# A hybrid attention block on one core: copies, ALiBi rows, a modulation sum, weight splits and the last output tile put elsewhere

## The chip, the cores and the metric

The kernel runs on one core of a Trainium2 chip. The metric is the device time of one execution in microseconds, taken as the median of several runs. Before the change it is 679.64 us, the median of three runs (677.84, 679.64, 680.59).

## The reference, cut to what matters

One transformer block on a sequence of 512 rows of width 1024, all in float32. A modulation vector is made from `c`; the mixer has six forget-gate attention heads ("fox"), four mLSTM heads and six block-sparse heads with ALiBi slopes ("moba"); then a gated feed-forward of width 2816.

```python
mod = silu(c) @ w_ada + b_ada
sh1, sc1, g1, sh2, sc2, g2 = split(mod, 6)
hn = rms(x, norm1_g) * (1 + sc1) + sh1
fq, fk, fv, ff, mq, mk, mv, mi, mf, mo, bq, bk, bv = split(hn @ w_in)
logf = log_sigmoid(f_pre); cum = cumsum(logf)      # fox and mLSTM gates
mq, mk = split(silu(causal_conv(concat(mq, mk))))
y = concat(fox(fq, fk, fv, cum), mlstm(mq, mk, mv, gates), moba(bq, bk, bv, slopes))
x = x + g1 * (y @ w_out)
hn = rms(x, norm2_g) * (1 + sc2) + sh2
gate, up = split(hn @ w_gate_up)
x = x + g2 * ((silu(gate) * up) @ w_down)
```

## The kernel before, in words

Every float32 product is made of three matmuls in a rounded type (fp32r): each operand is split into a high part (a copy into that type, usually on ACT) and a low part (the operand minus its high part, on DVE or on GpSimd, called POOL), and `mm3` (line 207) adds high x high, high x low and low x high. A name that ends in h or l is such a part. `wload` (line 235) loads a weight tile through SP's DMA queue, makes the high part on ACT and the low part on the engine that it is given. Stage buffers for weights rotate through four, split buffers through six.

**Stage 0** (lines 251 to 399) normalises `x`, makes the first modulation and the projection `gT[0..3]` of the mLSTM q|k channels. Its last lines copy the four PSUM banks to `qkz[0..3]`, in turn on ACT and DVE (lines 395 to 399).

**The mixer** (lines 401 to 986) is a list of groups of projection steps, written by `add_group` (line 410): A (mLSTM values and gates), F0, F1, F2 (fox), B0 to B2 (moba), E (output gate) and o0 (output projection). Each group has eight weight tiles `kt` and four row tiles `t`, one PSUM bank for each row tile; four banks with the tag "g" rotate, so that the first matmuls of F0 write the banks that group A used. A bank of A is empty when `after_a` (line 498) has read it: the gate sum into `gt` and, for two tiles `Vm0` and `Vm1`, a high part on ACT and a low part on DVE. The low part of a weight tile goes to POOL for `kt` in `WPG = (0, 2, 4, 6)`, except in group A (line 414).

Between these steps a queue of attention work runs: `plan_mlstm` and `plan_softmax`. What mLSTM needs first is the **gate chain**: `gates_1` (line 505, log-sigmoid as a row of small DVE steps on `gtmp` with an exponential on ACT, ending in `pre`), `gates_2` (cumulative sums `pF` on TensorE, then `Fc` and `ar` on DVE), `gates_3` (transpose `pR`, copy `rr`, running maximum `Mr`, and the table `RW` with high and low rows), and from `RW` the matmul `mb` that spreads a row over 128 partitions, from which the decay tiles `E` are made. `ms` and `mo` are the mLSTM score and value products.

`ada_all` (line 603) is a generator that makes later modulations beside this work: g1 (line 604, two halves named g10 and g11), sc2, sh2. Each half is eight loads of 128x512 and eight DVE steps that add a load times a column of `cs` to an accumulator (lines 566 to 581). `row_constants` (line 483) makes `sel` (a 0/1 table, built on POOL, cast on DVE) and the ALiBi rows `AL` (a DMA, a copy on ACT, a subtraction on DVE); it is called once, ahead of the step loop (line 929).

In this part the program order is not the order of issue: a scheduler places the instructions of every engine by their dependences, and each engine then runs its own list strictly in that order. `V, S, G, TE, SY` are thin wrappers (`_InOrder`, line 104) that can also chain instructions by hand.

**The second half** (from line 989) is the last output projection, the second norm and the feed-forward, and then the down projection `d`: two column halves of 512, four row tiles each, 22 weight tiles (line 1320 on). For the last four weight tiles the loop runs row tile by row tile, and after each row tile DVE multiplies the bank by `g1b` (here g2), adds `x1` and SP stores it. For the very last row tile these two DVE steps and the store are done in two halves of 256 columns, after all its matmuls.

Of the kernel before, what the change touches and what calls it, by code (L numbers as in the profile page):

```python
# [11 lines left out]
AF = mybir.ActivationFunctionType  # L12
# [46 lines left out]
DLAST = 4  # L59
# [44 lines left out]
class _InOrder:  # L104


    def __init__(self, tc, eng, on):
        self._tc, self._eng, self._on, self._last = tc, eng, on, None

    def __getattr__(self, name):  # L110
        f = getattr(self._eng, name)

        def call(*a, **k):
            r = f(*a, **k)  # L114
            ins = getattr(r, "ins", None)
            if ins is None or not self._on[0]:
                self._last = None
            else:
                if self._last is not None:
                    self._tc.add_manual_dep(  # L120
                        ins, self._last.name,
                        mybir.DependencyInfo(mybir.DependencyClass.NoSync, mybir.DependencyReason.DATA),
                        reason="issue order")
                self._last = ins
            return r

        return call
# [3 lines left out]
def hybrid_block_kernel(  # L131
# [75 lines left out]
    def mm3(o, ah, al, wh, wl, start, stop):  # L207
        TE.matmul(o, ah, wh, start=start, stop=False)
        TE.matmul(o, ah, wl, start=False, stop=False)
        TE.matmul(o, al, wh, start=False, stop=stop)  # L210
# [40 lines left out]
    with ExitStack() as s0:  # L251
# [143 lines left out]
        for m in range(4):  # L395
            if m % 2:
                V.tensor_copy(qkz[m], gT[m])
            else:
                S.activation(qkz[m], gT[m], AF.Copy)
# [10 lines left out]
    def add_group(name, kts, srcf, n, lhs, after, blk=BLK):  # L410
        box = {}

        def load(kt):
            box["w", kt] = wload(srcf(kt), n, f"{name}w{kt}", G if kt in WPG and name != "A" else V)
# [68 lines left out]
    def row_constants():  # L483
# [7 lines left out]
        V.tensor_copy(sel[0:64], sv)  # L491
# [74 lines left out]
    def ada_half(c0, name, bias):  # L566
        acc = adp.tile([P, 512], F32, tag="aacc", name=name, bufs=1)
        for k in range(8):
            s_ = adp.tile([P, 512], F32, tag="ast", name=f"{name}s{k}", bufs=AST)
            SY.dma_start(s_, w_ada_v[:, k, c0:c0 + 512])  # L570
            if k == 0:
                V.tensor_scalar(acc, s_, cs[:, 0:1], None, op0=ALU.mult)
            else:
# [357 lines left out]
    def g12():  # L931
        gs["lf"] = gates_1()

# [10 lines left out]
    for i in range(3):  # L944
# [3 lines left out]
             len(steps) - len(OKT) + 2: [load_x1]}  # L948
# [371 lines left out]
    for hf_ in range(2):  # L1320
        gg = [bank(tg, f"d{hf_}{t}") for t, tg in enumerate(("gggg", "sstt")[hf_])]

        def down(j, t, hf_=hf_, gg=gg):
# [9 lines left out]
            mm3(gg[t], ah[:, tsl], al[:, tsl], wh, wl, j == 0, j == NJ - 1)  # L1333
# [4 lines left out]
        for t in range(NT):  # L1338
            for j in range(NJ - DLAST, NJ):
                down(j, t)  # L1340
            parts = 2 if hf_ and t == NT - 1 else 1
            for c_ in range(parts):
                n = 512 // parts
                o = slice(c_ * n, c_ * n + n)
                ho = slice(512 * hf_ + c_ * n, 512 * hf_ + c_ * n + n)
# [43 lines left out]
```

## Time and profile before

| | before |
|---|---|
| median of three runs | 679.64 us |
| the profiled execution | 678.59 us |
| its span, first to last instruction | 676.8 us |
| TensorE matmul busy | 646.9 us, 96% |
| DVE busy | 518.1 us, 77% |
| ACT busy | 365.1 us, 54% |
| POOL busy | 97.2 us, 14% |
| mean granted TensorE clock | 0.995 |

The span counts from the first to the last instruction on the core; the execution's time has some 2 us more around it. Busy time of TensorE is modelled from pipelined matmuls. In the rows below, a name stands for all tiles of that name with their numbers left out (`F` for F0 to F2, `g` for g10 and g11, `E`, `ms`, `mo` for all heads); all program lines appear as L114, the wrapper's line. `PE` is TensorE, `PEld` its weight loads. A note in brackets at a row's end is the idle time ahead of it and what ended it.

### The profile page before, as it was taken

What the parts mean: (1) busy time and instruction counts of PE and PEld (TensorE: products, weight loads), DVE (VectorE), ACT (ScalarE), POOL (GpSimd) and SP (SyncE); (2) the same over time, 40 slices, a digit from 0 to 9 for tenths busy, and PEclk for the clock granted to TensorE, in tenths of its full rate; (3) what the DMA queues carried; (4) which work ended last, traced back from release to release, by engine and by line L of the source; (5) the groups of instructions that cost most, each with busy time, mean ns of one, the idle gap of its engine ahead of it and who ended that gap; (6) DMA issues with size and microseconds to landing.
All of it is one profiled execution on the core that took longest, in us unless ns stands there. A gap on an engine that the chain in (4) does not pass through costs nothing.

```text
span 676.8 us, 11779 instructions
## 1 busy us (share of the span) xinstructions
PE 646.9 (96%) x4238; PEld 588.9 (87%) x4238; DVE 518.1 (77%) x1034; ACT 365.1 (54%) x722; POOL 97.2 (14%) x135
## 2 busy tenths in 40 slices
PE   4999899999999999999999999999999999999997
PEld 3678888899999988778999999999999998788885
DVE  3549889969998899888778987888777999448313
ACT  4445478656876777645834554554544665316210
POOL 3012216344252355000000000000000000000000
PEclk9999988999999999999999999999999999999999
DMA  9986736667877667621346433322433237306101
GB/s 270 306 244 166 189 94 145 169 176 205 199 219 180 177 197 189 222 87 33 109 156 219 125 125 125 113 60 78 125 125 126 100 120 225 148 15 214 51 0 62
DMA packets 95549, 99.64 MB, mean 147 GB/s; under 512 B 8186, under 2 KB 70010, under 8 KB 95492
## 3 DMA queue, kind: packets, MB, share of 16 engines
q1 hardware_dynamic: 95492, 98.91, 50.3%
q8 instruction: 33, 0.54, 0.4%
q14 instruction: 24, 0.20, 0.1%
HBM read 84.15 MB, written 2.10 MB: 127 GB/s over the span
## 4 chain that ended last, share of the span: by engine, by line
PE 64%; DVE 19%; ACT 5%; DMA 5%; issue 4%; SPq 2%; POOL 0%; DVEq 0%; ACTq 0%; POOLq 0%
PE d L114 14%; PE B L114 5%; PE F L114 4%; PE ol L114 3%; PE gT L114 2%; DVE g L114 2%; SPq L114 2%; PE f9A L114 1%; PE f8A L114 1%; PE f7A L114 1%; PE f6A L114 1%; PE f5A L114 1%; PE f4A L114 1%; PE f3A L114 1%; PE pc L114 1%
## 5 line engine op out<-in xcount | busy, mean ns | idle before, releaser
L114 ACT ACTIVATE ah<-A 128x512 fp32r<-128x512 f32 x44 | 25.6, 620 | 33.4 <-PE d L114 33.1
L114 DVE TENSOR_TENSOR al<-A,ah 128x512 fp32r<-128x512 f32 x44 | 29.1, 685 | 18.1 <-ACT ah L114 18.1
L114 DVE TENSOR_TENSOR r<-r,r 128x1024 f32<-128x1024 f32 x20 | 24.4, 1220 | 1.5 <-DMA r<-in_w_gate_up_dram 1.2
L114 DVE TENSOR_TENSOR fo<-d,g1b 128x512 f32<-128x512 f32 (+1 forms) x9 | 5.6, 630 | 17.9 <-PE d L114 17.8
L114 ACT ACTIVATE Fp<-Fs,Fmn 128x128 f32<-128x128 f32 (+3 forms) x24 | 12.6, 526 | 9.8 <-DVE Fmn L114 5.6
L114 ACT ACTIVATE u<-u 128x512 f32<-128x512 f32 x20 | 12.5, 627 | 8.1 <-DVE u L114 8.0
L114 ACT ACTIVATE Bp<-Bs,Bmn 128x128 f32<-128x128 f32 (+3 forms) x24 | 12.6, 526 | 7.4 <-DVE Bmn L114 3.5
L114 DVE SCALAR_TENSOR_TENSOR m<-pc,b1sc,prmT 128x1 f32<-128x1 f32 x8 | 1.7, 218 | 19.1 <-PE pc L114 15.7
L114 POOL TENSOR_SCALAR Fp<-Fp,Fls 128x128 f32<-128x128 f32 (+2 forms) x18 | 11.1, 618 | 26.4 <-DVE Fls L114 21.3
L114 PE MATMUL gT<-sq,ident 128*128 128x256 f32 x12 | 5.3, 626 | 9.1 <-ACT sq L114 9.1
L114 DVE TENSOR_TENSOR A<-u,u 128x512 f32<-128x512 f32 x20 | 13.7, 684 | 0.0
L114 POOL TENSOR_SCALAR Bp<-Bp,Bls 128x128 f32<-128x128 f32 (+2 forms) x16 | 8.2, 510 | 34.4 <-DVE Bls L114 25.0
L114 DVE CUSTOM_DVE_ANT_0 Bs<-Bs,mask 128x128 f32<-128x128 f32 (+3 forms) x24 | 11.6, 492 | 1.6 <-PE Bs L114 1.6
L114 DVE TENSOR_TENSOR Bptl<-Bpt,Bpth 128x128 fp32r<-128x128 f32 (+3 forms) x24 | 11.5, 483 | 1.7 <-ACT Bpth L114 1.5
L114 ACT ACTIVATE Fpth<-Fpt 128x128 fp32r<-128x128 f32 (+3 forms) x24 | 10.4, 435 | 4.2 <-PE Fpt L114 4.1
L114 PEld LDWEIGHTS gT<-sq,ident 128*128 128x128 f32 x12 | 3.8, 329 | 10.0 <-issue 9.1
L114 DVE CUSTOM_DVE_ANT_0 Fs<-Fs,mask 128x128 f32<-128x128 f32 (+3 forms) x24 | 11.7, 488 | 1.0 <-PE Fs L114 1.0
L114 POOL TENSOR_TENSOR sml<-E,smh 128x512 fp32r<-128x512 f32 (+1 forms) x8 | 9.0, 1126 | 23.6 <-ACT smh L114 23.6
L114 PE MATMUL Bpt<-ident,Bp 128*128 128x128 f32 x60 | 10.8, 277 | 1.3 <-POOL gmo L114 0.5
L114 ACT ACTIVATE Bpth<-Bpt 128x128 fp32r<-128x128 f32 (+3 forms) x24 | 10.3, 433 | 3.2 <-PE Bpt L114 2.9
L114 DVE TENSOR_TENSOR Fptl<-Fpt,Fpth 128x128 fp32r<-128x128 f32 (+3 forms) x24 | 11.6, 484 | 0.5 <-ACT Fpth L114 0.4
L114 ACT ACTIVATE row<-pc 128x256 f32<-128x256 f32 x8 | 3.1, 382 | 15.7 <-PE pc L114 15.7
(2326 smaller groups left out, 2830.0 us busy)
## 6 DMA issues: line engine op xcount, KB each, us to landing
r<-in_w_gate_up_dram SPq DMA_DIRECT2D x40, 512.0 KB, 3.8
dr<-in_w_down_dram SPq DMA_DIRECT2D x22, 512.0 KB, 5.5
ada<-in_w_ada_dram SPq DMA_DIRECT2D x16, 512.0 KB, 7.2
x<-in_x_dram SPq DMA_DIRECT2D x4, 512.0 KB, 5.6
w0s<-in_w_in_dram SPq DMA_DIRECT2D x8, 256.0 KB, 6.6
g10s<-in_w_ada_dram SPq DMA_DIRECT2D x8, 256.0 KB, 3.6
g11s<-in_w_ada_dram SPq DMA_DIRECT2D x8, 256.0 KB, 2.7
sc20s<-in_w_ada_dram SPq DMA_DIRECT2D x8, 256.0 KB, 4.0
```

What stands on the lines that cost most here:

```text
L114: r = f(*a, **k)
```

## The change

Five edits. The copies of `qkz` and the cast of `sel` go to ACT altogether. The ALiBi rows become a function of their own, called in step 24 instead of ahead of the loop. The first step of a modulation half that comes after `gates_1` is bound to stand behind the last instruction of `gates_1` on DVE (`after`), which holds for g10. The low parts of F0's even weight tiles go from POOL to DVE. The last row tile of the down projection runs its last four weight tiles once for each half of 256 columns, each followed by its two DVE steps and its store.

```diff
     def __init__(self, tc, eng, on):
-        self._tc, self._eng, self._on, self._last = tc, eng, on, None
+        self._tc, self._eng, self._on, self._last, self._last_any = tc, eng, on, None, None
+
+    def after(self, first):
+        self._tc.add_manual_dep(
+            self._last_any, first.name,
+            mybir.DependencyInfo(mybir.DependencyClass.NoSync, mybir.DependencyReason.DATA),
+            reason="issue order")
...
         for m in range(4):
-            if m % 2:
-                V.tensor_copy(qkz[m], gT[m])
-            else:
-                S.activation(qkz[m], gT[m], AF.Copy)
+            S.activation(qkz[m], gT[m], AF.Copy)
...
-            box["w", kt] = wload(srcf(kt), n, f"{name}w{kt}", G if kt in WPG and name != "A" else V)
+            box["w", kt] = wload(srcf(kt), n, f"{name}w{kt}", G if kt in WPG and name not in ("A", "F0") else V)
...
-        V.tensor_copy(sel[0:64], sv)
+        S.activation(sel[0:64], sv, AF.Copy)
+
+    def alibi_rows():
         al = hp.tile([P, 512], F32, tag="P1", name="al", bufs=SB)
...
             if k == 0:
                 V.tensor_scalar(acc, s_, cs[:, 0:1], None, op0=ALU.mult)
+                if gs["last"] is not None:
+                    V.after(gs["last"])
+                    gs["last"] = None
...
     def g12():
         gs["lf"] = gates_1()
+        gs["last"] = V._last_any
...
-             len(steps) - len(OKT) + 2: [load_x1]}
+             len(steps) - len(OKT) + 2: [load_x1], 24: [alibi_rows]}
...
-        def down(j, t, hf_=hf_, gg=gg):
+        def down(j, t, o=slice(0, 512), hf_=hf_, gg=gg):
...
-            mm3(gg[t], ah[:, tsl], al[:, tsl], wh, wl, j == 0, j == NJ - 1)
+            mm3(gg[t][:, o], ah[:, tsl], al[:, tsl], wh[:, o], wl[:, o], j == 0, j == NJ - 1,
+                skip_group_check=hf_ * NT + t == 2 * NT - 1)
...
         for t in range(NT):
-            for j in range(NJ - DLAST, NJ):
-                down(j, t)
             parts = 2 if hf_ and t == NT - 1 else 1
             for c_ in range(parts):
                 n = 512 // parts
                 o = slice(c_ * n, c_ * n + n)
+                for j in range(NJ - DLAST, NJ):
+                    down(j, t, o)
```

As the scheduler answers to these edits, the lists of all engines differ between group A and the first fox heads, and are the same again from there to the last tile. Three places follow. First, DVE while group A's banks are emptied (`A0`, `A1` are the banks of A's first two row tiles; `gt` the gate sum), before:

```order
L114 TENSOR_TENSOR gt_578<-A0_651,gbias_83 128x14
L114 SCALAR_TENSOR_TENSOR g10_1029<-g10s3_1194,cs_84,g10_1029 128x512
L114 SCALAR_TENSOR_TENSOR mkl0_909<-qkz2_113,mkh0_908 128x512
L114 TENSOR_TENSOR Vm0_570<-A0_651,Vm0_570 128x2x64
L114 TENSOR_TENSOR gt_578<-A1_661,gbias_83 128x14
L114 SCALAR_TENSOR_TENSOR g10_1029<-g10s4_1227,cs_84,g10_1029 128x512
L114 TENSOR_TENSOR Vm1_571<-A0_651,Vm1_571 128x2x64
```

and now:

```order
L121 TENSOR_TENSOR gt_578<-A0_647,gbias_83 128x14
L121 TENSOR_TENSOR F0w2l_800<-F0w2s_797,F0w2h_799 128x384
L121 TENSOR_TENSOR Vm0_570<-A0_647,Vm0_570 128x2x64
L121 TENSOR_TENSOR mql0_903<-qkz0_111,mqh0_902 128x512
L121 TENSOR_TENSOR gt_578<-A1_657,gbias_83 128x14
L121 SCALAR_TENSOR_TENSOR mkl0_905<-qkz2_113,mkh0_904 128x512
L121 TENSOR_TENSOR Vm1_571<-A0_647,Vm1_571 128x2x64
```

The two g10 steps are gone from between the gate sum and the last read of A's first bank, a split of F0 has come, Vm0 stands ahead of mkl0, and mql0, which stood ahead of the first of these rows, is among them.

Second, DVE from the end of the log-sigmoid to the first decay tile, before:

```order
L114 TENSOR_TENSOR pre_860<-pre_860,gtmp_842 128x10
L114 COPY Fc_579<-pF_882 128x40
L114 TENSOR_TENSOR ar_580<-gt_578,Fc_579 128x4x4
L114 COPY ar_580<-Fc_579 128x4x6
L114 COPY rr_940<-pR_935 10x512
L114 SCALAR_TENSOR_TENSOR Mr_942<-rr_940 4x512
L114 TENSOR_TENSOR F0w7l_998<-F0w7s_995,F0w7h_997 128x384
L114 COPY rh_947<-RW_582 10x512
L114 TENSOR_TENSOR RW_582<-rr_940,rh_947 10x512
L114 TENSOR_TENSOR RW_582<-Mr_942,RW_582 4x512
```

and now, from `pre` to the scan `Mr`:

```order
L121 TENSOR_TENSOR pre_856<-pre_856,gtmp_838 128x10
L121 TENSOR_SCALAR g10_1025<-g10s0_1026,cs_84 128x512
L121 COPY Fc_579<-pF_878 128x40
L121 SCALAR_TENSOR_TENSOR g10_1025<-g10s1_1067,cs_84,g10_1025 128x512
L121 TENSOR_TENSOR ar_580<-gt_578,Fc_579 128x4x4
L121 COPY ar_580<-Fc_579 128x4x6
L121 SCALAR_TENSOR_TENSOR g10_1025<-g10s2_1115,cs_84,g10_1025 128x512
L121 COPY rr_936<-pR_931 10x512
L121 TENSOR_TENSOR F0w6l_955<-F0w6s_952,F0w6h_954 128x384
L121 SCALAR_TENSOR_TENSOR Mr_938<-rr_936 4x512
```

The first three g10 steps and the split F0w6l now stand inside this chain; before, the g10 steps s0 to s5 stood ahead of it, and s6 and s7 behind it.

Third, TensorE around the first `mb` (`F00` to `F03` are F0's four banks, one for each row tile), before:

```order
L114 MATMUL F03_931<-F0w4h_872,hn4l_104 128x384
L114 MATMUL mb0_962<-RW_582,sel_584 128x512
L114 MATMUL pM_982<-ident_61,Mr_942 128x4 x4
L114 MATMUL F00_835<-F0w5h_902,hn5h_105 128x384
L114 MATMUL F00_835<-F0w5l_903,hn5h_105 128x384
```

and now:

```order
L121 MATMUL F03_927<-F0w4h_868,hn4l_104 128x384
L121 MATMUL F00_831<-F0w5h_898,hn5h_105 128x384
L121 MATMUL F00_831<-F0w5l_899,hn5h_105 128x384
L121 MATMUL F00_831<-F0w5h_898,hn5l_106 128x384
L121 MATMUL F00_831<-F0w6h_954,hn6h_107 128x384
L121 MATMUL F00_831<-F0w6l_955,hn6h_107 128x384
L121 MATMUL F00_831<-F0w6h_954,hn6l_108 128x384
L121 MATMUL F00_831<-F0w7h_993,hn7h_109 128x384
L121 MATMUL mb0_958<-RW_582,sel_584 128x512
L121 MATMUL pM_978<-ident_61,Mr_938 128x4 x4
```

Seven matmuls of F0's first row tile have moved from behind `mb0` to ahead of it.

## Rows read from the trace of the kernel before

**Rows 1.** The page's first part: busy us (share of the span) x instructions.

```profile
PE 646.9 (96%) x4238; PEld 588.9 (87%) x4238; DVE 518.1 (77%) x1034; ACT 365.1 (54%) x722; POOL 97.2 (14%) x135
```

**Rows 2.** Busy time by stretch; columns: stretch, engines, granted clock, DMA share, GB/s.

```profile
84.00:128.00 44.00, 40.02 (x218) 36.69 (x219) 39.36 (x96) 33.32 (x87) 16.89 (x17) 0.92 0.50 128
84.00:90.00 6.00, 5.25 (x22) 5.03 (x23) 5.17 (x10) 2.30 (x7) 1.46 (x2) 0.72 0.60 170
105.00:110.00 5.00, 4.51 (x19) 4.37 (x18) 4.76 (x21) 4.92 (x9) 0.47 (x1) 0.66 0.70 168
128.00:155.00 27.00, 26.52 (x171) 25.23 (x171) 21.49 (x73) 16.21 (x51) 10.50 (x14) 1.00 0.69 179
```

**Rows 3.** TensorE's timeline, groups A and F0; columns: start us, us, instruction.

```profile
59.77 0.29 PE L114 MATMUL A<-Aw0h,hn0h 128*128 128x270 f32 x1
...
68.38 0.29 PE L114 MATMUL A<-Aw7h,hn7l 128*128 128x270 f32 x1
69.70 0.41 PE L114 MATMUL F<-F0w0h,hn0h 128*128 128x384 f32 x1 [1.03 <-DVE Vm L114]
...
84.75 0.47 PE L114 MATMUL mb<-RW,sel 128*128 128x512 f32 x1 [1.39 <-DVE RW L114]
```

**Rows 4.** The chain that ended last, merged; columns: start us, us, what.

```profile
85.55 3.01 PE F L114 x9
...
145.32 2.09 PE F L114 x12
...
379.96 2.88 PE f2A L114 x24
...
577.92 94.35 PE d L114 x416
```

**Rows 5.** DVE's timeline, from the ALiBi step to F0's weights.

```profile
58.71 0.68 DVE L114 TENSOR_TENSOR AL<-al,AL 6x512 fp32r<-6x512 f32 x1
...
66.07 0.74 DVE L114 SCALAR_TENSOR_TENSOR g<-g10s,cs,g 128x512 f32<-128x512 f32 x1
67.71 0.69 DVE L114 SCALAR_TENSOR_TENSOR mkl<-qkz,mkh 128x512 fp32r<-128x512 f32 x1 [0.90 <-ACT mkh L114]
...
69.82 0.55 DVE L114 TENSOR_TENSOR F0w3l<-F0w3s,F0w3h 128x384 fp32r<-128x384 f32 x1
```

**Rows 6.** ACT's timeline, from the q|k copies to F0's weights.

```profile
55.59 0.60 ACT L114 ACTIVATE qkz<-gT 128x512 f32<-128x512 f32 x1 [1.49 <-PE gT L114]
...
60.34 0.43 ACT L114 ACTIVATE Aw6h<-Aw6s 128x270 fp32r<-128x270 f32 x1 [0.96 <-PE A L114]
...
65.97 0.53 ACT L114 ACTIVATE F0w2h<-F0w2s 128x384 fp32r<-128x384 f32 x1 [0.63 <-DMA F0w2s<-in_w_in_dram]
```

**Rows 7.** DVE's timeline, the gate chain from the sums to RW.

```profile
78.36 0.20 DVE L114 COPY Fc<-pF 128x40 f32<-128x40 f32 x1 [1.59 <-PE pF L114]
...
79.66 0.68 DVE L114 COPY rr<-pR 10x512 f32<-10x512 f32 x1 [0.80 <-PE pR L114]
...
82.52 0.69 DVE L114 TENSOR_TENSOR RW<-rr,rh 10x512 fp32r<-10x512 f32 x1
83.23 1.37 DVE L114 TENSOR_TENSOR RW<-Mr,RW 4x512 fp32r<-4x512 f32 x1
```

**Rows 8.** DVE's timeline, two steps beside POOL.

```profile
62.76 1.50 DVE L114 SCALAR_TENSOR_TENSOR cy<-qkz,prmT,cy 128x510 f32<-128x510 f32 x1
...
90.84 1.78 DVE L114 TENSOR_TENSOR g<-g,g10b 1x512 f32<-1x512 f32 x1
```

**Rows 9.** DVE's timeline, the end of the program.

```profile
672.29 0.76 DVE L114 TENSOR_TENSOR fo<-d,g1b 128x256 f32<-128x256 f32 x2 [1.30 <-PE d L114]
672.96 0.75 DVE L114 TENSOR_TENSOR fo<-fo,x 128x256 f32<-128x256 f32 x2
```

More of the change, by code (lines that the diff above doesn't have):

```diff
@@ L115, in call @@
             ins = getattr(r, "ins", None)
+            self._last_any = ins or self._last_any
             if ins is None or not self._on[0]:
@@ L205, in rsqrt_, with mm3 @@
             f()
[L207 to L210, printed above, removed]
+    def mm3(o, ah, al, wh, wl, start, stop, **kw):
+        TE.matmul(o, ah, wh, start=start, stop=False, **kw)
+        TE.matmul(o, ah, wl, start=False, stop=False, **kw)
+        TE.matmul(o, al, wh, start=False, stop=stop, **kw)
     g1b = cp.tile([P, D], F32, name="g1b")
```

## The prediction, made before the changed kernel had run

> **What bounds the kernel now.** I read the page's shares first: TensorE is busy for 96% of the span and VectorE (DVE) for 77% [rows 1]. A share is a mean over stages, so the next view is the table by stretch. The second half (the feed-forward part) runs TensorE without a gap, and the change touches only its last tile; the rest of the change lies between 54 and 155 us. There both engines are nearly full [rows 2]: from 84 to 128 us DVE is busy 39.36 of 44 us, and TensorE has two stretches with a mean granted clock of 0.72 and 0.66, a mix of its two levels, 2.4 and 1.2 GHz. Then I read in TensorE's timeline what ends its idle times. Projection group F0 starts 1.03 us after group A's matmuls, because DVE had not emptied A's first PSUM bank. The matmul mb0 waits 1.39 us for the row table RW, which DVE writes at the end of the gate chain [rows 3]. Right after it, in the chain of waits, nine matmuls take 3.01 us, 0.33 each, where twelve of the same shape later take 2.09, 0.174 [rows 4]: half clock, after an idle time. Some eleven matmuls run so, 11 x 0.16 = 1.7 us lost, and the second low stretch loses about as much.
>
> **The change, part by part.**
>
> *Group A's banks.* From A's last matmul to F0's first there is a chain over two engines: gate sum, Vm's high part on ACT, its low part on DVE, for two tiles Vm0 and Vm1. On DVE two g10 steps (0.74 us, the next start 0.66 later) and mkl0 stand in it; mkl0 waits 0.90 us for ACT's mkh0 [rows 5], which is itself behind F0w2h, and that waits for its DMA until 65.97 [rows 6]. In the new order the g10 steps are gone from there, one split of 0.47 (F0w2l, priced by F0w3l, 0.55 with the next start 0.46 later [rows 5]) has come, Vm0's high part stands ahead of mkh0 on ACT, and on SP three g10 loads and the ALiBi load no longer stand among the weights. I chain the new order with the old durations: gate sum at 65.3, F0w2l done 65.9, Vm0 66.1, mql0 66.7, mkl0 67.45, Vm1 67.7: ahead of TensorE's last A matmul at 68.38 [rows 3]. All of 1.03 goes if F0w2 lands a microsecond sooner, 0.5 if it lands when it did. Taken: **-1.0** (0 to -1.2).
>
> *The gate chain up to RW.* The log-sigmoid starts at 70.2 instead of 70.9, since g10 has left DVE and the last gate sum follows TensorE; its small steps and the ACT table load keep their latencies, so its sum ends 0.8 us sooner. pF's matmuls then end at 77.2, and Fc comes at 77.25 instead of 78.36. Three g10 steps now stand in this chain: the first in the wait for pF (1.59 us before), free; the second between Fc and ar, on the path; the third in the wait for pR (0.80 us before), free [rows 7]. So: second g10 step to 78.1, ar 78.35, pR on TensorE, rr 79.1 to 79.75 (before, from 79.66), F0w6l, which POOL did before, to 80.2, the scan to 81.35, rh, F0w7l and the first RW step to 82.85, the last RW step to 83.5. Before, that last one took 1.37 us for four partitions, beside two POOL splits, where the step ahead of it took 0.69 [rows 7]; if POOL now meets another step of the chain, add that 0.7: 84.2. The old end was 84.6. TensorE's order now has seven F0 matmuls (7 x 0.174 = 1.2 us) ahead of mb0. It reaches mb0 at 83.2 - 1.0 + 1.2 = 83.4 and waits 0.1 to 0.8 where it waited 1.39. So mb0 comes 0.4 to 1.1 sooner with 1.2 us of later work done, 2.0 in the middle, of which 1.0 is the term above: **-1.0** (-0.6 to -1.3).
>
> *The rest of g10, from 84 to 128 us.* Three g10 steps (3 x 0.66 = 2.0 us) come into this stretch from before 73 us. What hides them is DVE's idle time there, 4.64 of 44 us [rows 2]; behind them wait the decay tiles E on DVE, and behind those TensorE's ms and mo products. With a start 2.0 us sooner most of it fits; if none of the idle time could be used, the whole 2.0 is lost. Taken: **+0.3** (0 to +2.0).
>
> A collision makes such a step dearer. A step of this kind (cy) took 1.50 us beside POOL's F0w0l, and g10's bias add on a single partition took 1.78 beside POOL's sml [rows 8], against the 0.74 of a g10 step alone [rows 5]. The Trainium skill (SBUF — State Buffer, Who interferes with whom) says that a VectorE instruction with two SBUF inputs and a GpSimd instruction that reads SBUF hold one shared port in turn, each for its whole length. The two rows agree with that; by it every g10 step placed among POOL's splits may wait a whole split, and the sum would be the second rival's below.
>
> *Four F0 splits from POOL to DVE* add 4 x 0.47 = 1.9 us to DVE before 83 us and take away the collision of 0.76 us at F0w0l. Two are in the chains above (F0w2l, F0w6l); F0w0l and F0w4l stand where DVE waits for TensorE's group A. Not counted again; if that cover were gone, 0.9.
>
> *q|k copies and sel to ACT.* ACT is idle for 1.49 us ahead of its first copy and 0.96 us a little later [rows 6]. The last copy ends near 57.7; its bank is wanted at 59.77 [rows 3]. Nothing; if ACT were late, conv starts one copy later, +0.5.
>
> *ALiBi rows.* The DVE step (0.68 us) leaves 58.71 us [rows 5] and comes to about 140, where DVE idles 5.5 us of 27 [rows 2]; the ACT step and the small load go with it. Nothing; +0.7 without that cover.
>
> *The last output tile.* DVE starts on the last bank at 672.29 with two multiplies and two adds of 256 columns, 0.42 each, and is done at 673.71 [rows 9]; the store follows. After the change the first half's pair runs beside the second half's matmuls. 24 of half width took 2.88 us in the feed-forward part, 12 of full width take 12 x 94.35 / 416 = 2.72 [rows 4]: +0.16. Then one multiply and one add, 0.04 between: 672.45 + 0.88 = 673.33. **-0.4** (0 to -0.8, as a store alone may be shorter).
>
> From 155 us on the order on every engine is the old one up to that tile, so a gain is carried to the end. Sum: -1.0 - 1.0 + 0.3 - 0.4 = **-2.1 us**. The profiled execution took 678.59 us (span 676.8), 1.05 under the median 679.64: 676.5 on its own scale, **677.5 us** on the median's.
>
> **The rivals.** *TensorE keeps its clock.* The first low stretch begins behind the wait at mb0 [rows 3, 4]. If that wait is short, 1.7 us more go, with the second stretch 3.4, provided DVE follows: its idle time there speaks for it, its 89% against. -3.8 to -5.5, that is 674.1 to 675.8; say 675.0.
>
> *DVE pays double, and it gets slower.* From 84 to 105 us the five late g10 steps meet POOL's sml and splits: three moved ones at 1.50, two old ones 0.76 dearer, 6.0 us in all, against 2.0 of earlier start and half the idle time, 2.3. +1.7 - 0.4 = +1.3: 680.9. It decides from 4.3 us of added DVE time on. [Rows 8] speak for it; against it, the g10 steps before ran beside little of POOL's work and POOL now has four splits less.
>
> *All is given back by 128 us.* DVE sets the pace, the three steps eat the earlier start, only the tail stays: -0.4, 679.2. DVE's 39.36 of 44 us speak for it, its idle time against.
>
> That the change does not do what it says is excluded by the order: g10 does stand behind the gate sum, and the last matmuls are halved.
>
> **The numbers.** Forecast 0.45, clock kept 0.25, given back 0.22, double price 0.08. 0.5% is 3.4 us, about what a measurement of this kernel can tell from no change. Faster by more: most of the clock case, 0.23, and the forecast at its better bounds, 0.07: 0.30. Slower by more: the double price with worse bounds, 0.06. Same: 0.64. The range reaches into both outer cases: 674.0 to 680.6.
>
> **What would show it.** F0's first matmul right behind A; mb0's wait at 0.8 us or less; the first E product at about 87.0 instead of 87.71; the first B0 matmul some 1.7 us before its old 155.05; two DVE steps behind the last matmul instead of four. It would be wrong if B0 starts when it did, if g10 steps of 1.5 us stand in DVE's timeline, or if the granted clock is 1.00 from 84 to 110 us.

## The result: slower by 0.67%, and the profile after

| | before | after |
|---|---|---|
| median of 22 runs | 677.45 us (675.34 to 680.59) | 681.97 us (679.04 to 685.83) |
| ratio, 95% interval | 1 | 1.0067 (1.0054 to 1.0080) |
| the profiled execution, its span | 678.59, 676.8 us | 683.67, 680.8 us |
| last A matmul to first B0 matmul | 68.38 to 155.05: 86.67 us | 68.48 to 160.70: 92.22 us |

The forecast was 677.5 against 679.64, faster by 0.3%. The kernel became slower by 0.67%. The result rests on 22 runs of each, so the median of before is another than that of the first three.

The loss stands where the change was made. In the profiled executions the first B0 matmul comes 5.65 us later, and the end of DVE's last step 4.20 later (677.91 against 673.71). In between, from the first B0 matmul to the row of 24 f2A matmuls in the chain that ended last [rows 4], the lists are the same, and this stretch took 224.91 us before and 222.79 after; over nineteen profiles it lies between 222.0 and 224.9, and the profile of before is the longest of them. So what follows compares distances from A's last matmul, not times from the start.

The page's first part of after, against [rows 1]:

```profile
PE 649.0 (95%) x4250; PEld 592.0 (87%) x4250; DVE 519.3 (76%) x1035; ACT 367.2 (54%) x725; POOL 93.1 (14%) x131
```

The busy times hardly moved: 2.1 us on TensorE, 1.2 on DVE. A loss of 4.5 us is therefore not work that was added, it is waiting and clock. The table by stretch of after, against [rows 2], and with the whole stretch from A to B0 as its last row:

```profile
84.00:128.00 44.00, 37.83 (x200) 35.17 (x200) 39.59 (x92) 31.82 (x79) 17.58 (x16) 0.88 0.51 132
...
128.00:155.00 27.00, 25.53 (x165) 24.52 (x164) 24.21 (x74) 16.93 (x52) 10.84 (x13) 1.00 0.73 195
...
68.48:160.70 92.22, 82.94 (x474) 77.36 (x472) 77.77 (x211) 58.06 (x155) 29.27 (x31) 0.93 0.61 160
```

The same stretch of before:

```profile
68.38:155.05 86.67, 80.54 (x474) 74.97 (x472) 73.42 (x210) 57.40 (x155) 30.91 (x33) 0.96 0.61 156
```

Both do the same 474 matmuls. The granted clock is a mix of the two levels 1.2 and 2.4 GHz, so a mean of 0.96 over 86.67 us is 2 x 0.04 x 86.67 = 6.9 us at the lower level, and 0.93 over 92.22 is 12.9. Half of such a time is lost, if TensorE is busy in it. The idle times that the trace puts in brackets on TensorE add up to 6.13 us before and 9.29 after. Waits and lost clock: 6.1 + 3.5 = 9.6 before, 9.3 + 6.5 = 15.7 after, a difference of 6.1 against the 5.55 seen, which is as near as a clock of two digits allows. About half of the loss is each.

TensorE's timeline of after (start us, us, instruction), against [rows 3], with a later wait and the last tile:

```profile
68.48 0.29 PE L121 MATMUL A<-Aw7h,hn7l 128*128 128x270 f32 x1
68.61 0.34 PE L121 MATMUL F<-F0w0h,hn0h 128*128 128x384 f32 x1
...
77.60 0.58 PE L121 MATMUL pF<-gtmp,tri 128*128 128x10 f32 x4 [1.45 <-DVE gtmp L121]
...
81.83 0.52 PE L121 MATMUL F<-F0w3h,hn3h 128*128 128x384 f32 x1
82.15 0.77 PE L121 MATMUL pR<-ident,ar 128*10 128x128 f32 x4
...
89.25 0.69 PE L121 MATMUL mb<-RW,sel 128*128 128x512 f32 x1 [2.32 <-DVE RW L121]
...
115.23 0.33 PE L121 MATMUL ms<-MIX,K 128*128 128x128 f32 x1 [2.56 <-DVE E L121]
...
674.51 0.28 PE L121 MATMUL d<-dw120h,al 128*128 128x256 f32 x1
...
675.31 0.39 PE L121 MATMUL d<-dw118h,ah 128*128 128x256 f32 x1 [0.52 <-DVE fo L121]
```

F0 starts right behind A; the wait of 1.03 is gone. But mb0 now comes 20.77 us behind A's last matmul instead of 16.37, and waits 2.32 for RW, which was to be 0.8 or less. The waits at 77.60, 115.23 and 675.31 had no counterpart of their length before.

Where the gate chain lost its time is read backwards on DVE, against [rows 7]:

```profile
71.66 0.49 DVE L121 TENSOR_TENSOR Vm<-A,Vm 128x128 fp32r<-128x128 f32 x2 [1.55 <-ACT Vm L121]
72.07 0.19 DVE L121 SCALAR_TENSOR_TENSOR gtmp<-gt 128x40 f32<-128x40 f32 x1
...
79.74 0.20 DVE L121 COPY Fc<-pF 128x40 f32<-128x40 f32 x1 [1.48 <-PE pF L121]
79.86 0.74 DVE L121 SCALAR_TENSOR_TENSOR g<-g10s,cs,g 128x512 f32<-128x512 f32 x1
80.52 0.17 DVE L121 TENSOR_TENSOR ar<-gt,Fc 128x16 f32<-128x16 f32 x1
...
83.03 0.68 DVE L121 COPY rr<-pR 10x512 f32<-10x512 f32 x1 [1.60 <-PE pR L121]
...
85.34 1.06 DVE L121 COPY rh<-RW 10x512 f32<-10x512 f32 x1
...
87.74 1.37 DVE L121 TENSOR_TENSOR RW<-Mr,RW 4x512 fp32r<-4x512 f32 x1
...
110.33 0.71 DVE L121 SCALAR_TENSOR_TENSOR n16a<-Frst,Fssq 128x16 f32<-128x16 f32 x1
...
114.53 0.18 DVE L121 SCALAR_TENSOR_TENSOR Frst<-n16b,Frst 128x16 f32<-128x16 f32 x1
114.62 0.55 DVE L121 TENSOR_TENSOR E<-ms,E 128x384 f32<-128x384 f32 x1
```

Two rows of before, beside [rows 7]:

```profile
70.88 0.42 DVE L114 SCALAR_TENSOR_TENSOR gtmp<-gt 128x40 f32<-128x40 f32 x1
...
78.59 0.18 DVE L114 TENSOR_TENSOR ar<-gt,Fc 128x16 f32<-128x16 f32 x1
```

Against before, counted from the start (A's last matmul is 0.10 later now), the first step of the log-sigmoid (`gtmp`) is 1.19 us late, Fc 1.38, ar 1.93, rr 3.37, RW's last step 4.51. Three steps of that staircase stand out: the wait of 1.55 for Vm's high part ahead of `gtmp` and the g10 step between Fc and ar, which are new, and the wait for `pR`, 1.60 instead of 0.80.

The first leads to ACT and from there to SP. ACT's timeline of after:

```profile
64.62 0.63 ACT L121 ACTIVATE mqh<-qkz 128x512 fp32r<-128x512 f32 x1
...
70.94 0.53 ACT L121 ACTIVATE F0w5h<-F0w5s 128x384 fp32r<-128x384 f32 x1 [1.51 <-DMA F0w5s<-in_w_in_dram]
71.37 0.42 ACT L121 ACTIVATE Vm<-A 128x128 fp32r<-128x128 f32 x2
...
72.48 1.28 ACT L121 ACT_TABLE_LOAD   x1
```

SP's issues in that stretch, after:

```profile
65.28 0.54 SPq L121 DMA_DIRECT2D MIX<-mqh  x1
65.93 0.52 SPq L121 DMA_DIRECT2D F0w4s<-in_w_in_dram  x1
66.96 0.37 SPq L121 DMA_DIRECT2D F0w5s<-in_w_in_dram  x1
```

and before:

```profile
64.24 0.58 SPq L114 DMA_DIRECT2D F0w4s<-in_w_in_dram  x1
64.92 0.43 SPq L114 DMA_DIRECT2D F0w5s<-in_w_in_dram  x1
65.41 0.53 SPq L114 DMA_DIRECT2D MIX<-mqh  x1
```

The transfer of `mqh0` into `MIX` has come ahead of two weight loads in SP's list. It waits for `mqh0`, an ACT step, and SP holds F0w4 and F0w5 behind it: F0w5 is issued at 66.96 instead of 64.92. `mqh0` itself is no later than before (its end is at 65.25, before at 65.34); what is new is that loads stand behind it. On ACT its high part F0w5h stands ahead of Vm's last high parts, so ACT waits 1.51 us for the DMA, DVE waits behind ACT, and the log-sigmoid behind DVE. TensorE then idles 1.45 us at pF, and the last F0w3 matmuls ahead of pR take 0.32 us each from start to start (81.83 to 82.15), where the same shape at full clock takes 0.174 [rows 4]: pR is late once more.

### The profile page after: what moved, and what is told of

Its sections match the earlier page's. It is cut to its first block, busy times and chain, and to the rows that moved or that the text cites. A ratio compares the mean times of both kernels' runs of the same rounds, so it can differ in the third digit from the quotient of the medians.

```text
span 680.8 us, 11805 instructions
## 1 busy us (share of the span) xinstructions
PE 649.0 (95%) x4250; PEld 592.0 (87%) x4250; DVE 519.3 (76%) x1035; ACT 367.2 (54%) x725; POOL 93.1 (14%) x131
## 4 chain that ended last, share of the span: by engine, by line
PE 66%; DVE 16%; DMA 6%; ACT 4%; issue 4%; SPq 2%; POOL 0%; DVEq 0%; ACTq 0%; POOLq 0%
PE d L121 14%; PE B L121 5%; PE fp L121 3%; PE ol L121 3%; PE F L121 3%; PE gT L121 3%; SPq L121 2%; DVE g L121 2%; PE f9A L121 1%; PE f8A L121 1%; PE f7A L121 1%; PE f6A L121 1%; PE f5A L121 1%; PE f4A L121 1%; PE f3A L121 1%
```

## The experiments

Two theories for most of the loss: the order on SP (loads late, and with them the whole gate chain), and the place of the g10 steps (DVE late, in the gate chain and behind it). Seventeen kernels, each with its ratio to before, are compared by five numbers. A to mb0 and A to B0 run from the start of A's last matmul; waits is the sum of TensorE's bracketed idle times between A and B0; clock is the mean granted clock there. The five come from one profiled execution each, the ratio from all timed runs.

| kernel | ratio (95%) | A to mb0 | A to B0 | waits | clock |
|---|---|---|---|---|---|
| before | 1 | 16.37 | 86.67 | 6.13 | 0.96 |
| the change | 1.0067 (1.0054 to 1.0080) | 20.77 | 92.22 | 9.29 | 0.93 |
| vm_first | 1.0053 (1.0032 to 1.0074) | 20.35 | 91.03 | 8.06 | 0.93 |
| sp_weights_first | 1.0022 (1.0001 to 1.0043) | 17.35 | 86.65 | 8.88 | 1.00 |
| g10_behind_ar | 1.0052 (1.0034 to 1.0070) | 20.29 | 90.79 | 7.31 | 0.92 |
| no_f0_split | 1.0051 (1.0031 to 1.0071) | 16.86 | 89.63 | 8.47 | 0.96 |
| loads_first_g10_free | 0.9995 (0.9980 to 1.0011) | 17.55 | 86.04 | 7.05 | 0.98 |
| tail_alone | 1.0011 (0.9995 to 1.0026) | 15.99 | 86.30 | 5.60 | 0.96 |
| g10_bind_alone | 1.0003 (0.9988 to 1.0018) | 17.17 | 85.38 | 6.21 | 0.98 |
| no_split_no_g10 | 1.0022 (1.0009 to 1.0035) | 17.87 | 88.08 | 7.28 | 0.96 |
| split_alone | 1.0005 (0.9994 to 1.0017) | 17.03 | 86.13 | 6.31 | 0.98 |
| best_no_tail | 0.9993 (0.9980 to 1.0005) | 17.29 | 85.77 | 6.67 | 0.98 |
| g10_free | 1.0044 (1.0023 to 1.0065) | 18.13 | 89.22 | 6.38 | 0.94 |
| pR_first | 1.0045 (1.0026 to 1.0064) | 18.91 | 89.67 | 8.58 | 0.96 |
| copies_as_before | 1.0021 (1.0000 to 1.0043) | 16.92 | 87.90 | 8.72 | 0.98 |
| split_loads_first | 1.0036 (1.0021 to 1.0051) | 18.13 | 88.92 | 6.22 | 0.94 |
| split_sel_alibi_loads_first | 0.9997 (0.9983 to 1.0011) | 16.80 | 88.14 | 7.76 | 0.96 |

The ratio follows A to B0 (correlation 0.92), less well A to mb0 (0.76): the loss is not all made ahead of mb0.

**The order on SP, and on ACT.** *sp_weights_first* binds the first thirteen transfers of this kind (`MIX<-mqh` is the first) behind F0w5's load on SP:

```diff
+    lastw = []
...
                 SY.dma_start(s_[:, o:o + w_].rearrange("p (a b) -> p a b", a=a.shape[1]), a)
+                if name == "F0w5":
+                    lastw.append(SY._last_any)
...
         SY.dma_start(f32(dst), f32(src))
+        if lastw and len(lastw) < 14:
+            SY.after(lastw[0])
+            lastw.append(None)
```

> The change with the stack DMAs of the first mLSTM pair bound behind F0w5's load on SP's list, as they stood before the change. Theory L: F0w4s and F0w5s are issued near 63.8 and 64.5 instead of 65.93 and 66.96, F0w5h no longer waits, the log-sigmoid starts at 70.2 to 70.5 instead of 72.07, TensorE does not idle for more than 0.3 us at pF and keeps its clock there, rr comes 2.5 to 3.5 us sooner (79.5 to 80.5), mb0 3 to 4.5 us sooner (85 to 86), and the time is 677.0 to 679.0. Theory G: the g10 steps still stand in the chain, so the time falls by 1.1 us at most: 680.9. Theory D: 681 to 682 with the first decay tile sooner and the first B0 matmul where it is.

TensorE's timeline of it:

```profile
76.95 0.58 PE L121 MATMUL pF<-gtmp,tri 128*128 128x10 f32 x4 [0.33 <-DVE gtmp L121]
...
86.52 0.47 PE L121 MATMUL mb<-RW,sel 128*128 128x512 f32 x1 [1.59 <-ACT F1w2h L121]
...
110.52 0.33 PE L121 MATMUL ms<-MIX,K 128*128 128x128 f32 x1 [2.56 <-DVE E L121]
```

mb0 comes 3.4 us sooner behind A than in the change, B0 5.6, and two thirds of the loss are gone (1.0067 to 1.0022). The wait at pF is 0.33 instead of 1.45. The wait for E is the same 2.56. All waits together are 8.88 us instead of 9.29, however: in this profile nearly all of the 5.6 us is clock, 1.00 instead of 0.93, and how an earlier gate chain keeps the clock up is not shown. A second profile of this kernel and of the change:

> A second look at the change with the stack DMAs behind F0w5's load, whose executions lie around 676.5 and around 680. Theory clock: where it takes more than 679, the trace shows TensorE at half clock in one or two stretches between 75 and 155 us that the first look (677.22, clock 1.00 there) has not, and the first B0 matmul 2 to 4 us later behind group A's last than its 86.65 us. Rival: the clock is the same and stage 0, ahead of group A, is what differs (its last matmul at 71 us or later instead of 69.17).

> A second look at the change itself, since its first look (683.67) lay above its median of 681.97. Theory L: F0w5h waits 1 us or more for its load, the log-sigmoid starts 3.0 us or more behind group A's last matmul, TensorE idles over 0.8 us at pF and over 1.5 us at mb0, and mb0 stands 19.5 us or more behind group A's last matmul (16.37 before). The clock may show one low stretch less than the four of the first look, and the time would be nearer to 682.

The first took 677.56 us, with A to mb0 17.86, A to B0 87.18, the second 681.22 us with 20.65 and 91.98 and the same wait of 2.56: the distances hold to half a microsecond from one execution to the next, the waits and the clock less well (7.93 us and 0.98, 9.95 us and 0.94).

*vm_first* leaves SP alone and puts F0w5h on ACT behind all but one of Vm's high parts:

```diff
+    vml = []
...
         S.activation(h_[:, :n], s_[:, :n], AF.Copy)
+        if name == "F0w5":
+            S.after(vml[0])
...
             S.activation(Vm[i][:, t, :, 0:64], src, AF.Copy)
+            if i == 0 and t == NT - 1:
+                vml.append(S._last_any)
```

> The change with one swap on ACT: the split F0w5h, which waited 1.51 us for its load, is bound behind Vm1 of A2 and Vm0 of A3; every other engine's list is the change's own. Theory L (the late log-sigmoid is the cause: it starts at 72.07 against 70.88 before, TensorE idles 1.45 us at pF, falls to half clock, and rr comes 3.4 us late): the log-sigmoid's first step starts near 70.4, but the table load on ACT still stands behind F0w5h, so pre ends 0.6 to 0.8 us sooner (77.0); TensorE's wait at pF falls to some 0.7 us. If the half clock then stays away, mb0 comes 2 us or more sooner and the time is 679.0 to 680.0; if it comes all the same, 681.0. Theory G (the g10 steps and F0w6l that stand in the gate chain are the cause): no more than the 0.7 us, 681.2. Theory D (DVE is too full from 84 to 128 us, whenever mb0 comes): no change, 682.0.

ACT's timeline of it:

```profile
71.17 0.52 ACT L121 ACTIVATE F0w5h<-F0w5s 128x384 fp32r<-128x384 f32 x1 [0.84 <-DMA F0w5s<-in_w_in_dram]
71.88 1.28 ACT L121 ACT_TABLE_LOAD   x1
```

The log-sigmoid's first step starts 1.6 us sooner behind A's last matmul (1.94 us instead of 3.59), but it then needs ACT's exponential, and the table load ahead of that still stands behind the late F0w5h: 71.88 instead of 72.48. mb0 gains 0.4 us. The late load has a second hold on the chain, which this swap leaves.

**Where g10 stands.** *g10_behind_ar* binds g10 behind `ar` instead of behind the log-sigmoid, which takes the 0.74 us step out from between Fc and ar:

```diff
     def g12():
         gs["lf"] = gates_1()
-        gs["last"] = V._last_any
...
     def g3():
         gates_2(*gs["lf"])
+        gs["last"] = V._last_any
```

> The change with g10's first step bound behind the last instruction of gates_2 instead of gates_1, so that no g10 step stands between pre and ar; two stand between ar and rr, in the wait for pR; F0w6l stays where it is, and pR comes three matmuls sooner in TensorE's list. Theory L: the log-sigmoid is as late as in the change (72.07), TensorE idles 1.45 us at pF and falls to half clock; ar comes 0.7 us sooner and rr 0.7 to 1.7 us sooner: 680.3 to 681.3. Theory G: most of the loss is gone, 678.0 to 679.0. Theory D: two g10 steps come later still into the crowded stretch, 682 to 683.

It is worth 0.5 us up to mb0 and 0.15% at the end, inside the interval. *g10_free* and *loads_first_g10_free* drop the binding, the second together with the order on SP of sp_weights_first:

```diff
     def g12():
         gs["lf"] = gates_1()
-        gs["last"] = V._last_any
+        gs["last"] = None
```

> The change without its binding of g10, the stack DMA still ahead of F0w4 and F0w5 on SP: the fourth corner of a square (stack first and g10 bound: 1.0067; loads first and g10 bound: 1.0022; loads first and g10 free: 0.9995). F0w6l stands ahead of rr in DVE's list, no g10 step between pre and the last RW row. Theory SP (the order of SP's list costs the 0.45% whatever g10 does): 1.004 or more, F0w5h waits for its load by 1 us. Theory G (the binding costs it, whatever SP does): 1.001 or less. Theory J (each is harmless alone, and only together do they push the gate chain past the point where TensorE runs dry at pF): 1.000 to 1.002, with F0w5h late but mb0 at 17 to 18 us behind group A's last matmul instead of 20.7.

> The change with the stack DMAs behind F0w5's load on SP, and without its binding of g10 (g10s0 to g10s6 stand ahead of pre on DVE again, three of them inside the log-sigmoid; F0's splits stay on DVE, with F0w6l ahead of the scan). Theory L+D (the loss has two parts: the late log-sigmoid through SP's order, which the run with the loads first gave back, and g10's steps moved into the stretch from 84 to 128 us, which is the rest): the rest goes too, 676.0 to 677.0 against 676.8 before, and the executions lie as close together as those of the kernel before. Theory L alone: no better than the run with the loads first, 678.0 to 678.5, or worse, as the g10 steps lengthen the log-sigmoid.

With the earlier runs these make a square: MIX first and g10 bound 1.0067, loads first 1.0022, g10 free 1.0044, both 0.9995. The order on SP is worth 0.45 to 0.49%, the binding 0.23 to 0.27%. Each of these differences is known to about 0.25, so the first is clear of noise, the second barely, and that they add is no more than what the medians say. Nor does the order act in one way: in g10_free F0w5h waits only 0.35 us for its load and the log-sigmoid starts 1.77 us behind A's last matmul, sooner than before (2.50). mb0 then comes 0.6 us later than in loads_first_g10_free; the other 2.6 us up to B0 are lost behind it, with the clock at 0.94 against 0.98. So the gate chain makes a fifth of the difference there, and what makes the rest is open.

With g10 free the wait of 2.56 at ms is gone, but shorter ones stand near its place, 1.68 us in loads_first_g10_free and this one in g10_free:

```profile
105.65 0.85 PE L121 MATMUL mo<-Vm,smh 128*128 128x130 f32 x3 [2.18 <-ACT F1w7h L121]
```

The 2.56 stands, 2.55 to 2.58 us long, in all nine profiles in which g10 is bound among other edits of the change. So this may be a second place of the loss, of less than its length. There DVE has, from 110.33 on, nine small steps of F0's norm, `mql` and two splits of F1 ahead of the E product at 114.62; before, that product stood ahead of them:

```profile
105.24 0.54 DVE L114 TENSOR_TENSOR E<-ms,E 128x384 f32<-128x384 f32 x1
```

DVE is no fuller there than before (39.59 of 44 us against 39.36); its order is another. That these steps cause the wait is read from the rows; no run moved them by themselves.

**The splits.** *no_f0_split* gives F0's low parts back to POOL:

```diff
-            box["w", kt] = wload(srcf(kt), n, f"{name}w{kt}", G if kt in WPG and name not in ("A", "F0") else V)
+            box["w", kt] = wload(srcf(kt), n, f"{name}w{kt}", G if kt in WPG and name != "A" else V)
```

> The change without its edit on the low parts of F0's even weights, which stay on POOL. In this order the loads F0w4 and F0w5 stand ahead of the stack DMAs on SP again, F0w5h stands behind Vm1 of A2 on ACT and ahead of Vm0 of A3, and F0w6l is not in DVE's gate chain; the g10 steps are. Theory L: the log-sigmoid starts within 0.5 us of 70.3, no idle time over 0.5 us at pF, 677.5 to 679.0. Theory G: F0w6l's 0.47 and its collision leave the chain, the g10 steps stay in it: 680.0 to 681.0. Theory D: POOL's four splits are back beside DVE's steps: 682 or more.

TensorE's timeline of it:

```profile
85.91 0.47 PE L121 MATMUL mb<-RW,sel 128*128 128x512 f32 x1 [1.54 <-DVE RW L121]
...
111.05 0.33 PE L121 MATMUL ms<-MIX,K 128*128 128x128 f32 x1 [2.58 <-DVE E L121]
```

This run speaks against late loads as the only cause. mb0 comes 16.86 us behind A, 0.5 more than before, and the kernel is still 0.51% slower. By B0 it is 2.96 us behind: the waits are 8.47 us instead of 6.13, the one for E among them, at the same clock of 0.96. *no_split_no_g10* is the same with g10 free and the loads first:

> The change without the edits on F0's splits and on g10, with the stack DMAs behind F0w5's load: the q|k copies and sel on ACT, the ALiBi rows late and the tail are left of it. Theory L+D: nothing that it names is left, and the time is the old one less the tail, 676.0 to 676.8, with 0.3 less if the DVE steps that went to ACT free group A's banks sooner. Theory C (one of these three small edits has a cost of its own, on ACT or on SP): 677.5 or more.

1.0022, where with the splits on DVE the same kernel has 0.9995. One DVE row of it shows what the old place of the splits costs when g10 is early again, against the 0.74 of a g10 step alone [rows 5]:

```profile
67.24 1.43 DVE L121 SCALAR_TENSOR_TENSOR g<-g10s,cs,g 128x512 f32<-128x512 f32 x1
```

**Single edits on the kernel before.** *split_alone* (the diff of no_f0_split turned round, on before), *g10_bind_alone* (the change's three g10 hunks) and *tail_alone* (its hunks on the last tile):

> The kernel before with the edit on F0's splits alone (DVE instead of POOL). In this order the first stack DMA stands ahead of F0w4 and F0w5 on SP, F0w5h ahead of Vm1 of A2 and Vm0 of A3 on ACT, and F0w6l between ar and rr on DVE; no g10 step stands between pre and ar. Theory L: F0w5h waits for its load by 1 us or more, the log-sigmoid's first step comes 1.0 us or more later after group A's last matmul than the 2.5 us before, TensorE idles at pF, and the time is 678.0 to 680.0 against 676.3. Theory G+D (it takes the g10 steps in the chain or behind it): F0w6l costs 0.5 us and the collisions on POOL's side go: 676.0 to 676.8.

> The kernel before with the binding of g10 behind the log-sigmoid alone. In this order the first stack DMA stands between F0w4 and F0w5 on SP, F0w5h ahead of Vm0 of A3 on ACT, and eight g10 steps behind pre on DVE. Theory L+D: the gate chain starts about as early as before or up to 0.5 us later, ar comes 0.7 us later by the g10 step ahead of it, and the stretch from 84 to 128 us holds DVE busy for 41 us or more of 44: 678.0 to 680.0. Theory L alone: within 0.5 us of the kernel before, 676.5 to 677.5. The forecast's own term for g10 (+0.3, with 1 us won ahead of it): 676.0 to 677.0.

> The kernel before with the edit of the last output tile alone; every list is the old one up to that tile. The forecast's term: -0.4 us (0 to -0.8), so 676.4 (676.0 to 676.8) against 676.8. In the trace two DVE steps stand behind the last matmul instead of two doubled ones, and from the last matmul's end to DVE's last step 0.91 us pass instead of 1.45; the 24 matmuls of half width take 0.1 to 0.2 us longer than the 12 did. Rival: the earlier store of the first half meets the second and nothing is won.

None of the three differs measurably from before (1.0005, 1.0003, 1.0011); so the binding has no price to be seen by itself, and neither have the splits. The q|k copies alone, and `sel` and the ALiBi rows alone, were not run. split_alone has the same SP order as the change, MIX ahead of the loads. If that order had a price of its own, it would be slower; it is not, and ACT shows why, since F0w5h waits for nothing:

```profile
69.36 0.53 ACT L121 ACTIVATE F0w5h<-F0w5s 128x384 fp32r<-128x384 f32 x1
```

F0w5 is issued there 2.14 us ahead of A's last matmul, in the change 1.52, before 3.46. From its issue to F0w5h's start 3.21 us pass there, 3.98 in the change. `mqh0` hardly differs: it ends 3.43 us ahead of A's last matmul there, 3.23 in the change. *copies_as_before* asks whether the copies on ACT have a share in the late load, giving two of the four `qkz` copies back to DVE in the whole change:

```diff
         for m in range(4):
-            S.activation(qkz[m], gT[m], AF.Copy)
+            if m % 2:
+                V.tensor_copy(qkz[m], gT[m])
+            else:
+                S.activation(qkz[m], gT[m], AF.Copy)
```

> The change with two of the four q|k copies back on DVE. In this order the stack DMA still stands ahead of F0w4 and F0w5 on SP, but F0w5h stands behind Vm1 of A2 on ACT, and the convolution's first ACT step comes ahead of two of the copies. Theory J: F0w5 is issued 0.3 us or more sooner against group A's last matmul (-1.5 us in the change), the log-sigmoid starts at 2.5 us or less behind that matmul instead of 3.5, and the ratio is 1.002 to 1.004. Rival: the copies have no share: F0w5h waits 1.2 us or more for its load as before, and the ratio is 1.006 or more.

ACT's and SP's timelines of it:

```profile
62.29 0.62 ACT L121 ACTIVATE mqh<-qkz 128x512 fp32r<-128x512 f32 x1
...
62.94 0.54 SPq L121 DMA_DIRECT2D MIX<-mqh  x1
...
64.61 0.37 SPq L121 DMA_DIRECT2D F0w5s<-in_w_in_dram  x1
```

MIX goes out at 62.94 instead of 65.28, F0w5 at 64.61 instead of 66.96, and the ratio is 1.0021, that of sp_weights_first. `mqh0` is sooner because ACT's list has it ahead of F0w1h here and behind it in the change, where F0w1h waits 1.48 us for its own load. So the late loads are undone either way, by MIX behind them or by an earlier `mqh0`. But the copies by themselves are not shown to make `mqh0` late: split_alone, without them, has it behind F0w1h too, and why its F0w5h finds its load there is seen only in part, in the 0.62 us of the issue and the shorter way. What is left (1.0021) has the wait of 2.58 for E in it.

*split_loads_first* and *split_sel_alibi_loads_first* put the loads first where the copies are still on DVE, the second with the `sel` and ALiBi edits too (diffs as above):

> The kernel before with the split edit alone and the stack DMAs behind F0w5's load. The split edit alone gave 1.0005 with the stack DMA ahead of F0w4 and F0w5; what it wins is that F0w0l, F0w2l, F0w4l and F0w6l no longer collide with DVE's steps and that group A's banks come free sooner. If SP's order costs something here too, the loads first give 0.1 to 0.3% back: 0.9975 to 0.9995, the best of all. Rival: the stack DMA costs nothing where the q|k copies are on DVE, since ACT's mqh0 is then early enough, and the ratio stays at 1.000 to 1.001.

> The same with sel on ACT and the ALiBi rows in step 24 as well; the copies, the tail and g10 are as before. If sel and the ALiBi step were in DVE's way ahead of group A's first splits, 0.1% better than the run without them; the forecast said nothing either way (0): 0.998 to 1.000.

The first is a miss: the order that saves 0.45% in the change costs 0.3% here (1.0005 to 1.0036), with A to mb0 1.1 us longer, the waits alike (6.22 and 6.31 us) and the clock at 0.94 instead of 0.98. The second is back at 0.9997. Prices found in one list do not hold in another.

**TensorE's order.** *pR_first* binds the transposes pR ahead of F0w3's matmuls, which had stood before them at half clock:

```diff
+            if self.first_after is not None:
+                self.after(self.first_after)
...
+        gs["pR"] = TE._last_any
...
         for f in extra.get(j, []):
             f()
+        if j in (11, 14):
+            TE.first_after = gs["pR"] if j == 11 else None
         half(1)
```

> The change with pR bound ahead of the F0w3 matmuls of F0's third and fourth row tiles in TensorE's list (in the change four of them stand ahead of pR, at half clock 1.3 us); mb0 stands four matmuls further ahead as well. Theory L: the log-sigmoid is as late as in the change, ar at 12.0 us behind group A's last matmul, but pR follows at 12.2 to 12.4 instead of 13.4 to 13.7, rr at 13.2 instead of 14.5, mb0 1.0 to 1.3 us sooner: 1.0045 to 1.0055. Rival: TensorE then only waits at pR instead of working, and the time stays at 1.006 to 1.007.

TensorE's timeline of it:

```profile
80.73 1.01 PE L123 MATMUL pR<-ident,ar 128*10 128x128 f32 x4
...
87.39 0.47 PE L123 MATMUL mb<-RW,sel 128*128 128x512 f32 x1 [0.96 <-DVE RW L123]
```

pR comes 1.4 us sooner and mb0 1.9, and the ratio falls by 0.22% to 1.0045, about what the two intervals can tell. It mends a consequence; the late start remains.

**The best of them.** *best_no_tail* is loads_first_g10_free without the halved last tile:

> The run with the loads first and g10 free (ratio 0.9995), now also without the edit of the last output tile. From g2p's matmul to DVE's last step the three kernels with that edit took 97.25 to 97.28 us, the two without it 96.89, since the second half's first matmul waits 0.52 us for DVE's multiply of the first half (the row names fo as its releaser). If that is right, this run takes 96.89 there and 0.37 us less in all: ratio 0.9990, 675.6 against 676.3. Rival: the tail's difference is within what executions differ by, and the ratio stays at 0.9995 or above.

0.9993, interval 0.9980 to 1.0005. No version beat the kernel before by more than its interval.

## Why the prediction was wrong, point by point

**Group A's banks (-1.0): right.** F0 starts 0.13 us behind A's last matmul, 1.32 before: -1.1 with A itself 0.1 later.

**The gate chain (-1.0): wrong, and this is the step that failed.** "The log-sigmoid starts at 70.2 instead of 70.9, since g10 has left DVE and the last gate sum follows TensorE" looked at DVE's list and TensorE's alone. It started at 72.07, because of a chain over SP (MIX ahead of F0w4 and F0w5), ACT (F0w5h ahead of Vm's high part) and DVE. Against the forecast 1.9 us are lost here, and since it starts 2.2 us behind A's last matmul instead of 3.6 with the loads first, most of this is the order's; then 0.74 for the g10 step ahead of `ar`, priced as such; then half clock ahead of pR; and `rh` and RW beside POOL. mb0 lies 4.40 us further behind A than before instead of 0.4 to 1.1 nearer. The term had no price for a wait on ACT or SP at all: the new SP list had been read for the loads that left it, not for the transfer that came forward.

**q|k copies to ACT (0, bound +0.5): wrong in its place.** "If ACT were late, conv starts one copy later" named the next user on TensorE. The price lay on SP, where two loads stand behind the transfer that waits for `mqh0`. `mqh0` is no later than before, but in the list that the scheduler makes with two of the copies on DVE it is 2.3 us sooner (62.29 instead of 64.62). Moving the transfer (sp_weights_first) and undoing the copies (copies_as_before) are each worth about 0.45%, 3 us.

**The rest of g10 (+0.3, 0 to +2.0): the size was off, and the cause seems another.** DVE's busy time in 84 to 128 us rose by 0.23 us only; the binding's price is 0.23 to 0.27%, 1.6 to 1.8 us, near the upper end, if it is one (it is barely clear of noise, and nothing by itself). The rows put it in the gate chain (g10_free brings mb0 2.6 us nearer to A) and at one E product that the scheduler had put behind a row of norm steps, not in a DVE that was full.

**Collisions with POOL: right in kind.** The last RW step took 1.37 us, as before and as allowed for; `rh` took 1.06 us, 0.42 before; one late g10 step took 1.78 against 0.74. The Trainium skill (SBUF — State Buffer, Who interferes with whom) gives the rule that the prediction weighed, and the RW and g10 rows, each a step with two inputs beside a POOL step, agree with it; `rh` has one input and is not a case of that rule. The two that are new are 0.64 + 1.04 = 1.7 us, not the 6.0 of the second rival. Two of the norm steps ahead of the E product also took 0.71 and 0.98 us beside POOL, the others 0.16 to 0.18.

**The last tile (-0.4): wrong.** The chain of waits of after and of before, from the last step ahead of the down projection:

```profile
580.65 1.10 PE g2p L121 x2
...
675.31 1.70 PE d L121 x12
```

```profile
576.82 1.10 PE g2p L114 x2
```

and DVE's end:

```profile
674.83 0.42 DVE L121 TENSOR_TENSOR fo<-d,g1b 128x256 f32<-128x256 f32 x1
675.28 0.42 DVE L121 TENSOR_TENSOR fo<-fo,x 128x256 f32<-128x256 f32 x1
677.03 0.42 DVE L121 TENSOR_TENSOR fo<-d,g1b 128x256 f32<-128x256 f32 x1 [1.32 <-PE d L121]
677.49 0.42 DVE L121 TENSOR_TENSOR fo<-fo,x 128x256 f32<-128x256 f32 x1
```

From g2p to DVE's last end it is 97.26 us, before 96.89 [rows 9]: +0.37 (97.24 to 97.28 in all thirteen profiles with this edit, 96.86 to 96.89 in the six without). DVE's end is shorter by 0.54, as forecast. But "the first half's pair runs beside the second half's matmuls" is not so: the second half's first matmul waits 0.52 us for the multiply of the first half to have read the bank, and starts 0.80 us behind the matmul ahead of it. The Trainium skill (PSUM — Partial Sum Buffer, PSUM bank collisions raise a hardware error) has a rule that spoke against this edit and was not weighed: two engines must be kept apart by bank, whichever columns they touch. The trace agrees with it: the matmul writes columns 256 to 511, DVE reads 0 to 255, and the program's semaphore holds the matmul until the read is over.

**The rivals.** None held. The second had the right sign, but its mechanism, late g10 steps beside POOL, gives a small part of the loss. None let the clock get worse, and the forecast had no term for that: it fell from 0.96 to 0.93 between A and B0, some 3 us. Of the marks named, F0 right behind A and the two DVE steps behind the last matmul came true; the first E product came at 93.31 instead of 87.0, and B0 5.65 us later instead of 1.7 sooner.

**Open.** Why TensorE falls to half clock behind one wait and not behind another is not settled: in the change it does behind 1.45 us, in the first profile of sp_weights_first it stays at 1.00 through waits of 1.59 and 2.56. So the half of the loss that is clock can't be assigned wait by wait. Nor is it settled why split_loads_first is slower than split_alone, or g10_free than loads_first_g10_free; in both pairs most of the difference is clock.

## What to carry to other kernels

Where an edit goes through a scheduler, compare the new lists of all engines, the DMA queue's above all, and look for what has come forward: a transfer that waits for a late producer holds every load behind it in its queue, and a late load can reach the critical chain through any engine on which its first user stands ahead of that chain. Take waits and granted clock apart before a wait is called the cause: in this kernel they weighed alike. Time such edits together and by pairs: here three of them did nothing measurable alone, and the price of the same order went from +0.45% to -0.3% with the rest of the list. An output tile cut within one PSUM bank did not win here, since the second half waits for the first half's read; a cut between banks was not run.

## What the hardware showed that was not expected

Executions of the same list differ ahead of the changed part: A's last matmul comes at 70.88 us in best_no_tail and at 68.50 in loads_first_g10_free, whose lists differ only in the last tile. And sp_weights_first ran between 675.92 and 681.69 us in twelve executions; its two profiles took 677.22 us, with the clock at 1.00 from A to B0, and 677.56, with 0.98 there, which is 2 x 0.02 x 87.18 = 3.5 us at the lower level.
